# Free words between four SBUF buffers of a decoder trunk kernel: which matmul operands lie at which distance

## The chip, the cores and the metric

The kernel runs on one core of one Trainium2 chip. The metric is the device time of one execution in microseconds, taken from repeated runs of the same program; the profile is of one further execution. TensorE (PE in the profile) multiplies: one operand, 128 x 128 at most, is held in the array after a weight load (PEld), the other, up to 512 columns, is moved through it. VectorE (DVE) and ScalarE (ACT) work element by element, GpSimd (POOL) does a little of the same, and SyncE (SP) issues the transfers. SBUF is the on-chip memory with 128 partitions; addresses below are bytes within a partition, the same in all of them.

## What is computed

Two layers on 256 tokens of width 2048. Each has a token mixer (a state-space mixer in layer 0, a causal convolution in layer 1) and a SwiGLU network of inner width 5632. The dense parts are

```python
vg = y @ w_glu                                   # 2048 -> 2 x 2048, layer 0
ab = u @ w_pw1                                   # 2048 -> 2 x 2048, layer 1
return jax.nn.silu(v) @ w_pw2                    # 2048 -> 2048,     layer 1

def swiglu_ffn(u, w_gu, w_down):                 # both layers
    gu = u @ w_gu                                # 2048 -> 2 x 5632
    g, v = jnp.split(gu, 2, axis=-1)
    return (jax.nn.silu(g) * v) @ w_down         # 5632 -> 2048
```

with a layer norm and a modulation by a projection of the conditioning vector (`ada_w`) between them. All data are float32.

## The kernel before

**Products in parts.** Each dense product is made of three products in a rounded 32-bit matmul format: an operand x is split into a high part (x rounded to that format) and a low part (x minus the high part), and hi x hi, hi x lo and lo x hi are added in PSUM. So every weight and every activation lies in SBUF twice. `Unit` (L822) loads 512 rows by 512 columns of weights into a `raw` buffer, ScalarE writes the high part to `whi` (L830) and VectorE the low part to `wlo` (L831). Both tiles are 4 x 512 words and have two buffers each in one pool, `w` (L1392).

**The activations.** `h` (L1265) holds the 2048 input channels of a product, high and low, as 16 chunks x 2 x 256 words; it is written once for each mixer or network and read by all its panels. `f` is the tile `f2` of `ffn` (L1220), 24 chunks x 2 x 256 words, in the pools `f0` (L1531) and `f1` (L1682); it holds the inner values of the network for the down projection, and under the name `raw` (`entry_raw`, L1501) the inputs of the first panel after a norm.

**Which operand is held.** `gemm` (L838) walks over the units of four 128-row chunks. In the wide form (L886) a 128-token piece of h or f is held and a 512-column row of `whi` or `wlo` is moved; a unit has 16 matmuls on `whi`, with the high and the low part of the activations, and 8 on `wlo`, with the high part. In the last panel of each product the form is narrow (L890): 128 columns of `whi` or `wlo` are held and 256 tokens of h or f are moved. The first panel after a norm (`Entry.panel`, L992) has matmuls of the narrow kind with 258 columns (L1007), from rows of 258 words. Transposes (L902) bring the results of wide matmuls back to channels by tokens.

**What sets the order.** Weights come on SyncE's queue, one unit ahead and more; `Later` and `AdaQueue` put the modulation's products on VectorE (L699) at a fixed rate beside the units. Nothing of this order depends on addresses.

**Where the buffers lie.** Pools are stacked: each begins where the pool opened before it ends. Reading the addresses from the program that is built from the kernel before:

| tile | first byte | modulo 512 |
|---|---|---|
| h | 38272 | 384 |
| whi, two buffers of 8192 | 113344 | 192 |
| wlo, two buffers of 8192 | 129728 | 192 |
| pool s (statistics, gates, temporaries) | 146112 | 192 |
| f | 177088 | 448 |

A chunk's piece in h or f has 512 bytes, a row of `whi` or `wlo` 2048, a held piece of weights 512. So for wide and narrow matmuls the distance from the held to the moving operand, modulo 512, depends on the four first bytes alone. Moving minus held is 320 (wide, h), 256 (wide, f), 192 (narrow, h) and 256 (narrow, f).

Of the kernel before, what the change touches and what calls it, by code (L numbers as in the profile page):

```python
# [11 lines left out]
F32 = mybir.dt.float32  # L12
F32R = mybir.dt.float32r
# [6 lines left out]
P = 128  # L20
# [485 lines left out]
def kernel(  # L506
# [69 lines left out]
    def load_unit(src, k0, kn, segs, eng=nc.sync):  # L576

        r = raws[0].tile([P, 4, 512], F32, tag="raw", name="raw")
        if kn > 4:
            r = r.rearrange("p a b -> p (a b)").rearrange("p (k n) -> p k n", k=kn)  # L580
        raws.append(raws.pop(0))
        at = 0
        for c0, n in segs:
            eng.dma_start(r[:, :kn, at:at + n], src[k0 * P:(k0 + kn) * P, c0:c0 + n].rearrange("(k p) n -> p k n", p=P))
            at += n
        return r

    class Later:


        def __init__(self):
            self.now, self.todo = 0, []
# [17 lines left out]
    def queue_behind(instructions):  # L610

        st = ExitStack()
        for i in instructions:
            st.enter_context(tc.issue_after(i.ins))
        return st
# [206 lines left out]
    class Unit:  # L822


        def __init__(self, wp, wsrc, k0, kn, segs, behind=()):
            r = load_unit(wsrc, k0, kn, segs)
            self.hi = wp.tile([P, 4, 512], F32R, tag="whi", name="whi")
            self.lo = wp.tile([P, 4, 512], F32R, tag="wlo", name="wlo")
            with queue_behind([*behind, *held_back]):
                m1 = nc.scalar.copy(out=self.hi[:, :kn], in_=r[:, :kn])  # L830
                m2 = nc.vector.tensor_tensor(out=self.lo[:, :kn], in0=r[:, :kn], in1=self.hi[:, :kn].bitcast(F32), op=SUB)  # L831
            self.marks = [m1, m2]
            nonlocal newest
            newest = self
# [480 lines left out]
    w = s5.work  # L1315
# [70 lines left out]
    raws[:] = [rawp] * 4 + [more.enter_context(tc.tile_pool(name="raw5", bufs=2))] * 2  # L1386
    mctx = ExitStack()

    def start_dense():
        nonlocal const2, wp  # L1390
        const2 = ctx.enter_context(tc.tile_pool(name="const2", bufs=1, reuse_waits="tile"))
        wp = mctx.enter_context(tc.tile_pool(name="w", bufs=2, reuse_waits="tile"))  # L1392
        ready.append(Unit(wp, s5_w_glu[0], 0, 4, [(0, 256), (D, 256)]))

    const2 = wp = ln_col = wtap = fold32 = row_of = None
# [14 lines left out]
    with tc.manual_schedule(engines={mybir.EngineType.PE}):  # L1410
# [9 lines left out]
        for ct in range(NCH - 1):  # L1420
            now, y = coming, None
            if (ct + 1) % 4 == 1 and ct < 12:
                load_x(ct // 4 + 1)
            s5.weights_in(ct + 1)
            n = plan[ct + 1]
            ada_units(n > 0)
            with queue_behind([] if ct else [s5.made]):
                tabs[ct + 1] = s5.tables(ct + 1, [last])
            if held:
                y = s5.read_out(*held)  # L1430
            u, uh, last = inputs(ct + 1)
            ada_units(n > 1)
            coming = ct + 1, u, s5.drive(ct + 1, uh)
            if not ct:
                s5.weights_out(0, d_col[:, 0:1], last)
            s5.weights_out(ct + 1, d_col[:, ct + 1:ct + 2], last)
            ada_units(n - 2)
            if ct == NCH - 2:
                raws[:] = [rawp]
                more.close()  # L1440
                s5.keep_ctx.close()
                start_dense()
            scan(ct, now, y)
            if ct % 4 == 3 and ct < 11:
                extra = quarter_steps(ct // 4 + 2)
            with queue_behind([s5.last]):
                next(extra, None)
# [61 lines left out]
    with mctx:  # L1509
        sp = mctx.enter_context(tc.tile_pool(name="s", bufs=1, reuse_waits="tile"))  # L1510
        sp_ada = mctx.enter_context(tc.tile_pool(name="ada", bufs=1, reuse_waits="tile"))
        stats = Stats("ln00", sp)

        def enter(name, stats, i, k, raw, pairs):
# [197 lines left out]
```

## Time and profile before

| | us |
|---|---|
| median of three runs | 2320.72 |
| lowest and highest of them | 2317.39, 2323.02 |
| profiled execution, whole | 2323.75 |
| profiled execution, span from first to last instruction | 2322.0 |
| TensorE busy in the span | 2249.4 |
| VectorE busy | 1633.0 |
| ScalarE busy | 1011.1 |

TensorE's granted clock was 0.992 of full speed on the mean, and 1.00 in all stages from about 450 us on but the convolution. DMA moved 251 GB/s on the mean. A row of a group of instructions reads: line, engine, operation, output and inputs by the program's names, shapes, count, busy time, mean ns of one, idle time before them and what ended it. Matmuls are pipelined, and a duration holds the depth of the pipeline: a wide matmul lasts some 390 ns though the next one starts some 230 ns after it. The step between two is read from their starts.

### The profile page before, as it was taken

To read this page: it belongs to the slowest core of one execution; us is meant where nothing else is said; L and a number is where in the kernel's file an instruction comes from. 1 tells how busy PE (TensorE), PEld (TensorE's weight loads), DVE (VectorE), ACT (ScalarE), POOL (GpSimd) and SP (SyncE) were. 2 spreads that over 40 slices of the span, in tenths; PEclk is the share of its full clock that TensorE was granted. 3 is DMA by queue.
4 is the path that set the end of the run, shared out by engine and by line. 5 is a ranking of instruction groups with operands and counts; after the bars stand their busy time and mean duration, and the time that the engine had idled before them with its cause. 6 is when DMAs were issued, how large, how long until landed. Compare 5 with 4: busy or idle time off the path is not lost.

```text
span 2322.0 us, 33968 instructions
## 1 busy us (share of the span) xinstructions
PE 2249.4 (97%) x13905; PEld 1811.9 (78%) x13905; DVE 1633.0 (70%) x1778; ACT 1011.1 (44%) x1242; POOL 186.6 (8%) x283
## 2 busy tenths in 40 slices
PE   6888999999999999999999998999999999999998
PEld 4545778988888888888897676798888888888888
DVE  8899878887777777777885565788754544555564
ACT  4666335554333334344453322556434333334343
POOL 5662000000000000000011111400000000000000
PEclk9999999999999999999999999999999999999999
DMA  9889799589888898988757886766865556555542
GB/s 334 289 301 302 268 320 337 168 304 323 294 321 294 314 318 294 324 293 318 274 164 222 265 241 193 276 223 206 275 218 187 193 182 197 184 182 189 191 164 91
DMA packets 382307, 582.35 MB, mean 251 GB/s; under 512 B 13604, under 2 KB 279124, under 8 KB 367684
## 3 DMA queue, kind: packets, MB, share of 16 engines
q1 hardware_dynamic: 381718, 579.73, 73.8%
q8 instruction: 109, 1.79, 0.3%
q0 software_dynamic: 192, 0.37, 0.1%
q14 instruction: 48, 0.39, 0.0%
q10 hardware_dynamic: 240, 0.08, 0.0%
HBM read 575.97 MB, written 4.15 MB: 250 GB/s over the span
## 4 chain that ended last, share of the span: by engine, by line
PE 82%; DVE 8%; DMA 4%; ACT 3%; issue 1%; POOL 1%; SPq 0%; DVEq 0%; ACTq 0%; POOLq 0%
PE acc L886 67%; PE acc L890 5%; PE conv L1608 2%; DVE wlo L831 2%; PE acc L1007 2%; PE turned L902 2%; DMA raw<-in_cv_w_pw_dram 1%; DMA raw<-in_s_w_glu_dram 1%; ACT whi L830 1%; DVE pin L462 1%; PE y L499 1%; PE ada L628 1%; DMA raw<-in_ada_w_dram 1%; DVE adaacc L699 1%; DVE x L450 0%
## 5 line engine op out<-in xcount | busy, mean ns | idle before, releaser
L831 DVE TENSOR_TENSOR wlo<-raw,whi 128x2048 fp32r<-128x2048 f32 x344 | 795.6, 2313 | 491.0 <-ACT whi L830 490.6
L830 ACT CAST whi<-raw 128x2048 fp32r<-128x2048 f32 x344 | 655.0, 1904 | 805.0 <-PE acc L886 579.1
L886 PE MATMUL acc<-whi,h 128*128 128x512 f32 x3648 | 895.0, 395 | 10.8 <-ACT whi L830 10.5
L886 PEld LDWEIGHTS acc<-whi,h 128*128 128x128 f32 x3648 | 679.4, 188 | 169.7 <-ACT whi L830 16.4
L886 PE MATMUL acc<-wlo,h 128*128 128x512 f32 x1824 | 466.1, 392 | 2.8 <-DVE wlo L831 2.8
L886 PEld LDWEIGHTS acc<-wlo,h 128*128 128x128 f32 x1824 | 341.6, 188 | 81.3 <-DVE wlo L831 6.7
L886 PE MATMUL acc<-whi,f 128*128 128x512 f32 x1248 | 300.5, 391 | 0.0
L699 DVE SCALAR_TENSOR_TENSOR adaacc<-rawa,c_act,adaacc 128x2048 f32<-128x2048 f32 (+1 forms) x135 | 284.5, 2108 | 0.4
L886 PEld LDWEIGHTS acc<-whi,f 128*128 128x128 f32 x1248 | 233.0, 188 | 48.9 <-ACT whi L830 0.8
L886 PE MATMUL acc<-wlo,f 128*128 128x512 f32 x624 | 156.4, 389 | 0.0
L886 PEld LDWEIGHTS acc<-wlo,f 128*128 128x128 f32 x624 | 117.1, 188 | 24.3
L1581 POOL TENSOR_TENSOR lw<-fold,wtap 128x1024 f32<-128x1024 f32 x16 | 33.7, 2110 | 1146.4 <-PE acc L890 926.4
L628 PE MATMUL ada<-raw,c_rep 128*32 128x512 f32 (+1 forms) x576 | 72.5, 600 | 5.7 <-DMA raw<-in_ada_w_dram 3.2
L1240 ACT ACTIVATE fsg<-acc 128x256 f32<-128x256 f32 x84 | 31.7, 380 | 100.0 <-PE acc L886 100.0
L890 PEld LDWEIGHTS acc<-h,whi 128*128 128x128 f32 x512 | 62.1, 190 | 8.1 <-DVE h L1637 2.6
L890 PE MATMUL acc<-h,whi 128*128 128x256 f32 x512 | 65.7, 283 | 2.6 <-DVE h L1637 1.7
L1184 POOL CAST lnmh<-lno 128x2 fp32r<-128x2 f32 x1 | 0.2, 183 | 829.3 <-DVE lno L66 829.3
L1608 PE MATMUL conv<-vs,lw 128*32 128x256 f32 x1024 | 59.8, 380 | 0.0
L1608 PEld LDWEIGHTS conv<-vs,lw 128*32 128x32 f32 x1024 | 36.7, 110 | 20.9 <-issue 3.0
L1241 DVE TENSOR_TENSOR fsg<-acc,fsg 128x256 f32<-128x256 f32 x84 | 35.1, 420 | 19.9 <-ACT fsg L1240 19.8
L462 DVE TENSOR_TENSOR_SCAN pin<-rho,pin 128x256 f32<-128x256 f32 x64 | 44.3, 692 | 1.5
L1617 DVE SCALAR_TENSOR_TENSOR V<-conv,vec,shift 128x256 f32<-128x256 f32 x14 | 9.7, 693 | 48.8 <-PE conv L1608 48.8
(331 smaller groups left out, 1829.8 us busy)
## 6 DMA issues: line engine op xcount, KB each, us to landing
raw<-in_ffn_w_gu_dram SPq DMA_DIRECT2D x352, 512.0 KB, 4.5
rawa<-in_ada_w_dram SPq DMA_DIRECT2D x128, 1024.0 KB, 5.9
raw<-in_ffn_w_down_dram SPq DMA_DIRECT2D x88, 1024.0 KB, 5.1
raw<-in_ada_w_dram SPq DMA_DIRECT2D x64, 1024.0 KB, 7.8
raw<-in_s_w_glu_dram SPq DMA_DIRECT2D x64, 512.0 KB, 6.0
raw<-in_cv_w_pw_dram SPq DMA_DIRECT2D x64, 512.0 KB, 6.3
raw<-in_cv_w_pw_dram SPq DMA_DIRECT2D x16, 1024.0 KB, 5.6
vs<-scr SPq DMA_DIRECT2D x28, 284.0 KB, 7.4
```

The lines of the kernel that those rows point to most:

```text
L462: v.tensor_tensor_scan(out=z, data0=rh[:, a].rearrange("p r h c -> p (r h c)"), data1=z, initial=0.0, op0=MUL, op1=ADD)
L628: nc.tensor.matmul(acc[32 * (k % 4):32 * (k % 4) + 32, :], c_rep[:, kk, :], r[:, k, :], start=kk < 4, stop=kk >= NCH - 4)
L699: nc.vector.scalar_tensor_tensor(out=acc, in0=r[:, i], scalar=c_act[:, kk:kk + 1], in1=acc, op0=MUL, op1=ADD)
L830: m1 = nc.scalar.copy(out=self.hi[:, :kn], in_=r[:, :kn])
L831: m2 = nc.vector.tensor_tensor(out=self.lo[:, :kn], in0=r[:, :kn], in1=self.hi[:, :kn].bitcast(F32), op=SUB)
L886: nc.tensor.matmul(acc[bank].rearrange("p a b -> p (a b)"), x[:, bank * HALF:(bank + 1) * HALF], wt[:, k], start=first, stop=end)
L890: nc.tensor.matmul(acc[bank][:, i], wt[:, k, m * P:(m + 1) * P], x, start=first and i == 0, stop=end and i == 1)
L902: nc.tensor.transpose(b[:, o:o + HALF], u[t][:, c0 + k * P:c0 + (k + 1) * P], ident)
L1007: nc.tensor.matmul(acc[m][:, 0:EW], wt[:, k, m * P:(m + 1) * P], xx[:, 4 * u + k], start=u == 0 and n == 0, stop=u == 3 and n == len(order ...
L1241: nc.vector.tensor_tensor(out=t[:, i], in0=gv[:, 0], in1=t[:, i], op=MUL)
L1581: nc.gpsimd.tensor_tensor(out=lw, in0=fold32.unsqueeze(1).unsqueeze(1).broadcast_to([P, 4, CONV_G, 32]), in1=bc(wtap[:, :, 4 * ch:4 * ch + ...
L1608: nc.tensor.matmul(acc[32 * q:32 * q + 32, :], lw[:, q, g, :], vs[:, q, 4 * g:4 * g + SEQ], start=g == 0, stop=g == CONV_G - 1)
```

## The change

Three tiles that nobody writes or reads are put between pools: 48 words (192 bytes) before the pool of `whi`, 16 words (64 bytes) between `whi` and `wlo`, which get a pool each, and 16 words between the pool `ada` and the pools of f. Everything else in the kernel is as before.

```diff
         def __init__(self, wp, wsrc, k0, kn, segs, behind=()):
             r = load_unit(wsrc, k0, kn, segs)
-            self.hi = wp.tile([P, 4, 512], F32R, tag="whi", name="whi")
-            self.lo = wp.tile([P, 4, 512], F32R, tag="wlo", name="wlo")
+            self.hi = wp[0].tile([P, 4, 512], F32R, tag="whi", name="whi")
+            self.lo = wp[1].tile([P, 4, 512], F32R, tag="wlo", name="wlo")
...
+    def gap(c, n):
+
+        gaps.append(f"gap{len(gaps)}")
+        c.enter_context(tc.tile_pool(name=gaps[-1], bufs=1)).tile([P, n], F32, name=gaps[-1])
+
+    gaps = []
+
     def start_dense():
         nonlocal const2, wp
         const2 = ctx.enter_context(tc.tile_pool(name="const2", bufs=1, reuse_waits="tile"))
-        wp = mctx.enter_context(tc.tile_pool(name="w", bufs=2, reuse_waits="tile"))
+        gap(ctx, 48)
+        wp = [mctx.enter_context(tc.tile_pool(name="whi", bufs=2, reuse_waits="tile"))]
+        gap(mctx, 16)
+        wp.append(mctx.enter_context(tc.tile_pool(name="wlo", bufs=2, reuse_waits="tile")))
         ready.append(Unit(wp, s5_w_glu[0], 0, 4, [(0, 256), (D, 256)]))
...
         sp = mctx.enter_context(tc.tile_pool(name="s", bufs=1, reuse_waits="tile"))
         sp_ada = mctx.enter_context(tc.tile_pool(name="ada", bufs=1, reuse_waits="tile"))
+        gap(mctx, 16)
         stats = Stats("ln00", sp)
```

By the sizes of the free tiles, whi then begins at 113536, wlo at 129984, the pool s at 146368 and f at 177408; h stays at 38272.

## The prediction

> **What bounds the kernel now.** I read the page first: busy shares, then the chain of work that ended last; then the groups of instructions by shape, for the matmuls; then the timeline of TensorE, for the step from one matmul's start to the next; last the busy time by stage.
>
> ```profile
> span 2322.0 us, 33968 instructions
> ...
> PE 2249.4 (97%) x13905; PEld 1811.9 (78%) x13905; DVE 1633.0 (70%) x1778; ACT 1011.1 (44%) x1242; POOL 186.6 (8%) x283
> ...
> PE 82%; DVE 8%; DMA 4%; ACT 3%; issue 1%; POOL 1%; SPq 0%; DVEq 0%; ACTq 0%; POOLq 0%
> PE acc L886 67%; PE acc L890 5%; PE conv L1608 2%; DVE wlo L831 2%; PE acc L1007 2%; PE turned L902 2%; DMA raw<-in_cv_w_pw_dram 1%; DMA raw<-in_s_w_glu_dram 1%; ACT whi L830 1%; DVE pin L462 1%; PE y L499 1%; PE ada L628 1%; DMA raw<-in_ada_w_dram 1%; DVE adaacc L699 1%; DVE x L450 0%
> ```
>
> TensorE is busy for 97% of the span and holds 82% of the chain, and 67% of the chain is one line, L886: the wide matmuls, whose held operand is a 128-column piece of h or f and whose moving operand is a 512-column row of whi or wlo. So what counts is the step between two of them. The groups by shape (line, engine, operation, tiles, form, count, then busy time and mean ns of one) give the counts:
>
> ```profile
> L886 PE MATMUL acc<-whi,h 128*128 128x512 f32 x3648 | 895.0, 395 | 10.8 <-ACT whi L830 10.5
> L886 PE MATMUL acc<-wlo,h 128*128 128x512 f32 x1824 | 466.1, 392 | 2.8 <-DVE wlo L831 2.8
> L886 PE MATMUL acc<-whi,f 128*128 128x512 f32 x1248 | 300.5, 391 | 0.0
> L886 PE MATMUL acc<-wlo,f 128*128 128x512 f32 x624 | 156.4, 389 | 0.0
> L890 PE MATMUL acc<-h,whi 128*128 128x256 f32 x512 | 65.7, 283 | 2.6 <-DVE h L1637 1.7 <-ACT whi L830 0.7
> ...
> L890 PE MATMUL acc<-f,whi 128*128 128x256 f32 x320 | 40.7, 284 | 0.0
> L890 PE MATMUL acc<-h,wlo 128*128 128x256 f32 x256 | 33.6, 281 | 4.6 <-DVE wlo L831 4.6
> L1007 PE MATMUL acc<-raw,whi 128*128 128x258 f32 x256 | 33.3, 284 | 0.0
> ...
> L890 PE MATMUL acc<-f,wlo 128*128 128x256 f32 x160 | 21.2, 283 | 0.0
> ```
>
> Wide: 3648 + 1824 = 5472 on h and 1248 + 624 = 1872 on f. Narrow (L890, weights held, activations moving): 768 on h, 480 on f. One matmul's duration holds a pipeline's depth, so the step is read from starts. TensorE's timeline in the down projection (f held), start, us and count of each merged row:
>
> ```profile
> 708.06 1.98 PE L886 MATMUL acc<-wlo,f 128*128 128x512 f32 x8
> 709.87 3.79 PE L886 MATMUL acc<-whi,f 128*128 128x512 f32 x16
> 713.50 1.98 PE L886 MATMUL acc<-wlo,f 128*128 128x512 f32 x8
> 715.31 3.79 PE L886 MATMUL acc<-whi,f 128*128 128x512 f32 x16
> 718.94 1.98 PE L886 MATMUL acc<-wlo,f 128*128 128x512 f32 x8
> 720.75 1.98 PE L886 MATMUL acc<-whi,f 128*128 128x512 f32 x8
> ```
>
> From 708.06 to 720.75 are 56 matmuls in 12.69 us, a step of 226.6 ns. The same in the up projection (h held):
>
> ```profile
> 907.52 1.99 PE L886 MATMUL acc<-wlo,h 128*128 128x512 f32 x8
> 909.35 3.83 PE L886 MATMUL acc<-whi,h 128*128 128x512 f32 x16
> 913.01 1.99 PE L886 MATMUL acc<-wlo,h 128*128 128x512 f32 x8
> 914.84 1.99 PE L886 MATMUL acc<-whi,h 128*128 128x512 f32 x8
> 916.67 1.08 PE L886 MATMUL acc<-wlo,h 128*128 128x512 f32 x4
> 917.59 1.99 PE L886 MATMUL acc<-whi,h 128*128 128x512 f32 x8
> 919.42 1.08 PE L886 MATMUL acc<-wlo,h 128*128 128x512 f32 x4
> 920.34 3.83 PE L886 MATMUL acc<-whi,h 128*128 128x512 f32 x16
> 924.00 1.30 PE L886 MATMUL acc<-wlo,h 128*128 128x512 f32 x5
> ```
>
> From 907.52 to 924.00 are 72 matmuls in 16.48 us: 228.9 ns. Same shape, same clock, nobody waits, and 2.3 ns more. What differs is where the held operand lies. From the program's own allocation, bytes modulo 512: h 384, whi and wlo 192, f 448. So moving minus held is 320 for h and 256 for f, in every wide matmul, since all other offsets are multiples of 512. Narrow matmuls tell the same, with h moving (distance 192; the first two rows) and f moving (256):
>
> ```profile
> 1382.82 3.57 PE L890 MATMUL acc<-h,whi 128*128 128x256 f32 x30
> 1386.22 1.98 PE L890 MATMUL acc<-h,wlo 128*128 128x256 f32 x16
> ```
>
> ```profile
> 2280.76 2.80 PE L890 MATMUL acc<-f,whi 128*128 128x256 f32 x22
> 2283.40 2.08 PE L890 MATMUL acc<-f,wlo 128*128 128x256 f32 x16
> ```
>
> 3.40 us for 30 is 113.3 ns; 2.64 us for 22 is 120.0 ns. And 113.3 for 256 columns is half of 226.6 for 512: the two good cases agree on 0.443 ns a column. I take that for the floor of this data path; h in the wide form lies 2.3 ns above it, f in the narrow form 6.7.
>
> **The change, part by part.** No instruction, DMA, queue or order is added, removed or moved; there is no new wait. The three free tiles have 48, 16 and 16 words; nobody writes or reads them. whi moves by 192 bytes, wlo by 256, the f pool by 320; h stays. New residues: h 384, whi 384, wlo 448, f 256. Moving minus held becomes, in the wide form, whi on h 0, wlo on h 64, whi on f 128, wlo on f 192; in the narrow form h against whi 0, h against wlo 448, f against whi 384, f against wlo 320. Not one of the four wide distances occurs in the wide form of the trace of before, so their cost is unknown and is bounded from both sides.
>
> Better side: every wide matmul at the floor. On h 5472 x (228.9 - 226.6) = 12.6 us; f is there already, 0. Narrow f, 480 x 6.7 = 3.2 us; narrow h is at the floor in the row shown. Together 15.8 us. The panels (L1007) move 258 columns with rows of 258 words, so their distances wander through the residues before and after; I put 0.
>
> Worse side: the one step seen between a good and a bad distance is 120.0 - 113.3 = 6.7 ns per matmul. If all wide ones pay it, they come at 226.6 + 6.7 = 233.3: h 5472 x 4.4 = 24.1 us, f 1872 x 6.7 = 12.5 us, 36.6 us in all. By pair that is 16.1 (whi on h), 8.0 (wlo on h), 8.4 (whi on f), 4.2 (wlo on f).
>
> I take the floor for the wide pairs on h, because of the two wide distances seen one is at it and the other only 2.3 ns off, and because 128 columns are loaded there while 512 stream, against 256 in the narrow form: the wide one has more room. For f I take no change, for narrow ones none. How much of 12.6 us reaches the end is read by stage (window, its length, busy us and count of PE, PEld, DVE, ACT, POOL, granted clock, DMA share):
>
> ```profile
> 230.00:390.00 160.00, 155.48 (x733) 121.47 (x731) 135.39 (x118) 56.93 (x49) 3.03 (x2) 0.99 0.89 308
> ...
> 690.00:835.00 145.00, 145.00 (x664) 119.35 (x663) 105.19 (x66) 53.79 (x34) 0.00 (x0) 1.00 0.87 312
> 835.00:1060.00 225.00, 225.00 (x1013) 182.85 (x1013) 169.47 (x125) 87.70 (x72) 0.00 (x0) 1.00 0.87 306
> ```
>
> From 690 on TensorE has no hole, so a shorter step is a shorter span; DMA at 0.87 has 13% spare against 1% that a faster step asks. In the first dense stage it waits 4.5 us in 160, so about a tenth of the wide work sits where the gain may turn into a wait. 12.6 less some 1.5 is 11 us.
>
> One more part: DVE and ScalarE read and write the moved tiles. Residues of raw (384) and whi come to coincide in the subtraction on L831.
>
> ```profile
> L831 DVE TENSOR_TENSOR wlo<-raw,whi 128x2048 fp32r<-128x2048 f32 x344 | 795.6, 2313 | 491.0 <-ACT whi L830 490.6
> L699 DVE SCALAR_TENSOR_TENSOR adaacc<-rawa,c_act,adaacc 128x2048 f32<-128x2048 f32 x105 | 246.1, 2344 | 0.0
> ```
>
> L699 reads as many elements from two SBUF tiles at another distance (64 against 192) and takes 31 ns more: at most 344 x 31 = 10.7 us either way on an engine that idles 30% of the span, hidden behind the matmuls wherever PE has no hole. If that cover were gone, as in the first dense stage, a tenth of it, 1 us, would show. I put 0.
>
> **Sum.** The profiled execution took 2323.75 us (span 2322.0, 1.75 around it), 3.0 above the median of 2320.72. Less 11 gives 2312.8 for that execution and 2309.7 beside the median: 2310.
>
> **Rivals.** (1) *Distance is no cause.* The 2.3 ns could come from something else that h and f do not share, or the pairs may win and lose about the same: then 2321, between 2316 and 2326. The Trainium skill, "TensorE: Matmul & The Clock Gate", section "Step-by-step: what each phase is for", says that loading the next weights does not steal read bandwidth from the running matmul; "SBUF — State Buffer", section "Who interferes with whom", that PE waits on nobody. By those the layout is worth 0 us and the time stays 2321. Against it stand 120.0 and 113.3 ns for one instruction form, both with no wait; for it, that no run here moved one tile alone. That the free tiles are laid out otherwise than named falls here too.
>
> (2) *A collision on every wide matmul: slower.* The mechanism: while a row of the weights streams, the next piece of h or f is read; where both meet in the same part of the 512 bytes the stream stops for 6.7 ns, as in the narrow f rows. It decides pair by pair. whi on h alone costs 16 us (2337), both f pairs alone 12.5 (2333), all four 36.6 (2357). Speaking for it: f now sits at the floor and can only lose, and hi and lo, now at one distance, get two, so that at 16 and 8 matmuls the pattern has to settle anew. Against: 2.3 ns is the worst wide case seen. It becomes a loss once whi on h is off the floor by more than it is now.
>
> (3) *The floor is lower still.* Then both wide pairs gain. No row shows a 512-column step under 226.6, and half of it in another form agrees, so I price it by that agreement's error only: each ns under the floor is worth 7344 x 0.001 = 7.3 us, 2302 with the gain on h. The skill's "Back-to-back issue gap" on the same TensorE page gives N / 2.4 + 2.5 ns, 215.8 for 512 columns; by it an estimate would be 7344 x 10.8 = 79 us more, and no run here shows it.
>
> **Chances.** Forecast, wide on h at or near the floor (2303 to 2315): 0.42. Rival 1: 0.25. Rival 2: 0.25, most of it under 2340. Rival 3: 0.08. The range 2300 to 2340 holds the forecast, rival 1 and the cheaper half of rival 2, some 0.8. A measurement of this kernel tells 0.2%, about 4.6 us, from no change: faster 0.50 (forecast and rival 3), same 0.25, slower 0.25.
>
> **What would show it.** In the timeline of after, 24 wide matmuls from whi to the next whi take 5.44 us at the floor, 5.49 as now, 5.60 with a collision each, to be read for h and f apart; 30 narrow ones take 3.40 or 3.60. Mean durations of the four L886 groups move with it, by the same nanoseconds. Counts, DMA sizes and waits must be the same. The prediction is wrong if the step on h stays at 228.9, if the step on f rises, or if the gain on TensorE reappears as idle time before L886.

## The result and the profile after

The changed kernel takes 2335.70 us (median of 4 runs, 2332.44 to 2338.44); the kernel before, beside it, 2320.21 (4 runs, 2317.39 to 2323.02). The ratio is 1.0066, with a 95% interval of 1.0048 to 1.0084: **slower by 15.5 us**, 0.7%. The time lies in the range given; the forecast direction was wrong. The profiled execution of after took 2332.44 us, 3.3 under its median, where that of before, with 2323.75, lay 3.5 above this one (3.0 above the median of three that it was first set beside); so the two spans, 2322.0 and 2330.7, differ by only 8.7.

The page of after, the same lines as of before:

```profile
span 2330.7 us, 33968 instructions
...
PE 2263.3 (97%) x13905; PEld 1813.4 (78%) x13905; DVE 1634.5 (70%) x1778; ACT 1012.8 (43%) x1242; POOL 186.2 (8%) x283
...
PE 83%; DVE 9%; ACT 2%; DMA 2%; issue 2%; POOL 1%; SPq 0%; DVEq 0%; ACTq 0%; POOLq 0%
PE acc L886 67%; PE acc L890 5%; PE conv L1619 3%; DVE wlo L831 2%; PE acc L1007 2%; PE turned L902 2%; DVE pin L462 1%; ACT whi L830 1%; DVE adaacc L699 1%; PE y L499 1%; DMA raw<-in_s_w_glu_dram 1%; DMA raw<-in_cv_w_pw_dram 1%; PE ada L628 1%; DMA raw<-in_ada_w_dram 1%; DVE x L450 0%
```

Every count is the one of before, and the bound is the same. TensorE is busy 13.9 us longer (2263.3 - 2249.4) and idle 5.2 us less (67.4 against 72.6). That before idles more goes with the one execution of it that was profiled: a kernel with the same distances, shifted by 512 bytes (below), has 66.9 us of it in a span of 2316.7, and against that trace after is busy 13.5 us longer and idle 0.5 us longer.

```profile
PE 2249.8 (97%) x13905; PEld 1811.0 (78%) x13905; DVE 1632.6 (70%) x1778; ACT 1010.4 (44%) x1242; POOL 186.0 (8%) x283
```

So no wait has taken the place of another: the matmuls themselves come more slowly. The groups of TensorE by shape (line, engine, operation, tiles, form, count, then busy us and mean ns of one, then idle time and its releasers) show which:

```profile
L886 PE MATMUL acc<-whi,h 128*128 128x512 f32 x3648 | 890.3, 393 | 8.0 <-ACT whi L830 7.7
L886 PE MATMUL acc<-wlo,h 128*128 128x512 f32 x1824 | 471.1, 395 | 2.9 <-DVE wlo L831 2.9
L886 PE MATMUL acc<-whi,f 128*128 128x512 f32 x1248 | 306.6, 396 | 0.0
L886 PE MATMUL acc<-wlo,f 128*128 128x512 f32 x624 | 160.1, 394 | 0.0
...
L890 PE MATMUL acc<-h,whi 128*128 128x256 f32 x512 | 68.0, 288 | 2.0 <-DVE h L1648 1.0 <-ACT whi L830 0.9
...
L890 PE MATMUL acc<-f,whi 128*128 128x256 f32 x320 | 40.3, 283 | 0.0
...
L890 PE MATMUL acc<-h,wlo 128*128 128x256 f32 x256 | 34.1, 284 | 4.3 <-DVE wlo L831 4.3
...
L890 PE MATMUL acc<-f,wlo 128*128 128x256 f32 x160 | 20.8, 280 | 0.0
```

Beside before's rows, whi on h went from 395 to 393 ns, wlo on h from 392 to 395, whi on f from 391 to 396, wlo on f from 389 to 394, narrow h against whi from 283 to 288 and against wlo from 281 to 284. One wide pair gained and three lost; of the narrow pairs those with h lost, and those with f gained a little (284 to 283 and 283 to 280). The timeline of TensorE (start us, length us, then the group and its count) gives the steps. In the down projection, f held:

```profile
709.29 2.03 PE L886 MATMUL acc<-wlo,f 128*128 128x512 f32 x8
711.16 3.88 PE L886 MATMUL acc<-whi,f 128*128 128x512 f32 x16
714.87 2.03 PE L886 MATMUL acc<-wlo,f 128*128 128x512 f32 x8
```

From 709.29 to 714.87 are 24 matmuls in 5.58 us, 232.5 ns each where they were 226.6. In the up projection, h held:

```profile
907.92 3.80 PE L886 MATMUL acc<-whi,h 128*128 128x512 f32 x16
911.56 2.01 PE L886 MATMUL acc<-wlo,h 128*128 128x512 f32 x8
913.41 1.99 PE L886 MATMUL acc<-whi,h 128*128 128x512 f32 x8
915.23 1.10 PE L886 MATMUL acc<-wlo,h 128*128 128x512 f32 x4
916.17 2.00 PE L886 MATMUL acc<-whi,h 128*128 128x512 f32 x8
918.01 1.10 PE L886 MATMUL acc<-wlo,h 128*128 128x512 f32 x4
918.94 3.81 PE L886 MATMUL acc<-whi,h 128*128 128x512 f32 x16
```

The first 16 on whi take 3.64 us, 227.5 ns each, nearly the floor. The next 8 on wlo take 1.85 us, 231.3 ns, above the 228.9 of before; the two runs of 4 take 0.94 and 0.93, about 234. So the cost is highest in the first matmuls after a change from whi to wlo, and where the runs are short these are all there are.

A mean step for each pair, for all of the trace, can be worked out from the starts of successive matmuls. A wide matmul's step runs to the start of the next wide one, whichever pair that belongs to; a narrow one's runs from the start of the narrow one before it. Steps of 260 ns and more are left out, so that waits and other work between them stay out. For the narrow form this limit is wide, and some waits stay in. The whole account of the change is this:

| pair | count | distance before, after | step before, ns | step after, ns | count x difference, us |
|---|---|---|---|---|---|
| wide, whi on h | 3648 | 320, 0 | 229.27 | 228.54 | -2.7 |
| wide, wlo on h | 1824 | 320, 64 | 228.90 | 231.83 | +5.3 |
| wide, whi on f | 1248 | 256, 128 | 227.20 | 232.21 | +6.3 |
| wide, wlo on f | 624 | 256, 192 | 226.68 | 232.85 | +3.9 |
| narrow, h against whi | 512 | 192, 0 | 119.31 | 124.51 | +2.7 |
| narrow, h against wlo | 256 | 192, 448 | 118.99 | 119.82 | +0.2 |
| narrow, f against whi | 320 | 256, 384 | 120.94 | 119.75 | -0.4 |
| narrow, f against wlo | 160 | 256, 320 | 120.00 | 117.91 | -0.3 |

The sum is +15.0 us, against 15.5 measured. With steps under 160 ns alone narrow h against whi goes from 115.9 to 119.8, worth 2.0 us and not 2.7; the kernel shifted by 512 bytes has 114.5 there, at the distance of before. So the narrow rows of the table are known to a microsecond or so, the wide ones better: between before and the shifted kernel their steps agree within 0.1 ns.

### The profile page after: what moved, and what is told of

The parts are those of the page before. It is cut to its first block, busy times and chain, and to the rows that moved or that the text cites. A ratio compares the mean times of both kernels' runs of the same rounds, so it can differ in the third digit from the quotient of the medians.

```text
span 2330.7 us, 33968 instructions
## 1 busy us (share of the span) xinstructions
PE 2263.3 (97%) x13905; PEld 1813.4 (78%) x13905; DVE 1634.5 (70%) x1778; ACT 1012.8 (43%) x1242; POOL 186.2 (8%) x283
## 4 chain that ended last, share of the span: by engine, by line
PE 83%; DVE 9%; ACT 2%; DMA 2%; issue 2%; POOL 1%; SPq 0%; DVEq 0%; ACTq 0%; POOLq 0%
PE acc L886 67%; PE acc L890 5%; PE conv L1619 3%; DVE wlo L831 2%; PE acc L1007 2%; PE turned L902 2%; DVE pin L462 1%; ACT whi L830 1%; DVE adaacc L699 1%; PE y L499 1%; DMA raw<-in_s_w_glu_dram 1%; DMA raw<-in_cv_w_pw_dram 1%; PE ada L628 1%; DMA raw<-in_ada_w_dram 1%; DVE x L450 0%
## 5 line engine op out<-in xcount | busy, mean ns | idle before, releaser
L831 DVE TENSOR_TENSOR wlo<-raw,whi 128x2048 fp32r<-128x2048 f32 x344 | 795.6, 2313 | 495.1 <-ACT whi L830 492.9
L886 PE MATMUL acc<-wlo,h 128*128 128x512 f32 x1824 | 471.1, 395 | 2.9 <-DVE wlo L831 2.9
L886 PE MATMUL acc<-whi,f 128*128 128x512 f32 x1248 | 306.6, 396 | 0.0
L886 PEld LDWEIGHTS acc<-whi,f 128*128 128x128 f32 x1248 | 233.7, 188 | 54.6 <-ACT whi L830 0.8
```

Of the source, the lines that this page charges most:

```text
L886: nc.tensor.matmul(acc[bank].rearrange("p a b -> p (a b)"), x[:, bank * HALF:(bank + 1) * HALF], wt[:, k], start=first, stop=end)
```

## The experiments

Three theories stood to be told apart. First, that the step depends on the **distance** from held to moving operand, pair by pair, with some period. Second, that it depends on something else that the free words move with them: the absolute place, or the pools being separate. Third, that two distances in alternation cost something **as such**, whatever they are. (A fourth stood in the expectations of the first runs, that any shift of the weights against h costs; the first run below, which is faster, ends it.) In all kernels the weights have a pool each and `gap` is as in the change; only the numbers of free words differ (ahead of whi, between whi and wlo, ahead of f), but for the last one. The short diffs are against the changed kernel. Steps in the tables are worked out as above.

**Only the first gap.** h and f keep one distance each: 0 for h, 256 for f.

```diff
         gap(ctx, 48)
...
-        gap(mctx, 16)
         wp.append(mctx.enter_context(tc.tile_pool(name="wlo", bufs=2, reuse_waits="tile")))
...
-        gap(mctx, 16)
         stats = Stats("ln00", sp)
```

> Only the 48 words before whi are left of the change. Residues: h 384, whi and wlo 384, f 128; moving minus held in the wide form 0 on h, 256 on f. Theory A (the residue of moving minus held modulo 512 sets the step; 0 and 256 settle at 226.7 ns in the traces of after and before): every wide matmul at 226.7 ns, so 5472 x (228.9 - 226.7) = 12 us below the kernel before, less up to 3 us because narrow matmuls on h go from 113 to 118 ns to some 120; about 2310. Theory B (the loss comes from giving whi and wlo two distances, whatever they are): as the kernel before, 2320. Theory C (any shift of the weights against h costs): slower than before, up to 2335.

Measured: 2312.37 us against 2318.78, ratio 0.9979 (0.9970 to 0.9989): this part alone is 6.4 us **faster**. Its timeline with h held:

```profile
908.07 1.98 PE L886 MATMUL acc<-whi,h 128*128 128x512 f32 x8
909.89 1.07 PE L886 MATMUL acc<-wlo,h 128*128 128x512 f32 x4
910.79 1.98 PE L886 MATMUL acc<-whi,h 128*128 128x512 f32 x8
912.61 1.07 PE L886 MATMUL acc<-wlo,h 128*128 128x512 f32 x4
913.51 3.79 PE L886 MATMUL acc<-whi,h 128*128 128x512 f32 x16
```

24 matmuls from 908.07 to 913.51 take 5.44 us, 226.7 ns: distance 0 is at the floor, and without a second distance the runs of 4 are at it too. The wide pairs on h gain 3648 x 1.75 + 1824 x 2.01 = 10.1 us by their mean steps (227.52 and 226.89), and narrow h gives back 512 x 5.2 + 256 x 3.7 = 3.6 (3.0 by the steps under 160 ns).

**Only the last gap.** f moves by 64 bytes, h and the weights lie as before; f's distance becomes 192, h's stays 320.

```diff
-        gap(ctx, 48)
...
-        gap(mctx, 16)
         wp.append(mctx.enter_context(tc.tile_pool(name="wlo", bufs=2, reuse_waits="tile")))
...
         gap(mctx, 16)
         stats = Stats("ln00", sp)
```

> Only the 16 words before the pools of f are left of the change. Residues: h 384, whi and wlo 192, f 0; moving minus held 320 on h as before, 192 on f for whi and wlo alike. Theory A: wide matmuls on h stay at 228.9 ns, those on f go from 226.7 to the 233.3 ns that wlo shows on f in the trace of after: 1872 x 6.6 = 12.4 us slower, narrow ones on f between 113 and 120 ns instead of 120, up to 3 us back; 2330 to 2333. Theory B (two distances for whi and wlo cost): no change, 2320. Theory C (only the weights against h matter): no change.

Measured: 2330.89 against 2318.78, 1.0054 (1.0042 to 1.0066), 12.1 us slower. Its timeline with f held:

```profile
706.51 3.89 PE L886 MATMUL acc<-whi,f 128*128 128x512 f32 x16
710.25 2.03 PE L886 MATMUL acc<-wlo,f 128*128 128x512 f32 x8
712.12 3.89 PE L886 MATMUL acc<-whi,f 128*128 128x512 f32 x16
```

24 matmuls in 5.61 us, 233.8 ns by these rounded starts; the mean over the trace is 233.3 on both whi and wlo. The steps on h stay at 229.3 and 228.9. By the steps, f costs 1248 x 6.12 + 624 x 6.63 = 11.8 us. Of the operands of the wide matmuls only f was moved here, which is the held one (the pool of the convolution, opened behind the same gap, moved with it); the matmuls that hold f slowed, and no others of the wide ones.

**All by 512 bytes** (`gap(ctx, 128)`, no other gap): the distances of before, at other places and in separate pools.

```diff
-        gap(ctx, 48)
+        gap(ctx, 128)
...
-        gap(mctx, 16)
...
-        gap(mctx, 16)
```

> One gap of 128 words (512 bytes) before whi and none else: all addresses of weights, pool s and f move, every distance modulo 512 is that of the kernel before. Theory A: each wide step as before, 228.9 on h and 226.7 on f, time 2320 within 5 us. If the period were 1024 or more, or if absolute addresses counted, steps on h and on f against the weights could change (f moves along with the weights, h does not): then the step on h leaves 228.9 and that on f stays.

Measured: 2318.51 against 2318.78, 1.0004 (0.9995 to 1.0014); wide steps 229.27, 228.86, 227.18 and 226.71, those of before. Separate pools and a free tile cost nothing by themselves.

**Distance 256 for both** (`gap(ctx, 112)`, no other gap): h and f both at 256, which before had for f alone.

```diff
-        gap(ctx, 48)
+        gap(ctx, 112)
...
-        gap(mctx, 16)
...
-        gap(mctx, 16)
```

> One gap of 112 words before whi. Residues: h 384, whi and wlo 128, f 384; moving minus held 256 in all wide pairs and in all narrow pairs. Theory A: all wide matmuls at 226.7 ns (12 us less than before), all narrow ones at 120.0 ns (768 on h from 113 to 118 up to 120, 3 us more): about 2311. Theory B: as before, 2320. Theory C: slower than before.

Measured: 2312.63 against 2318.78, 0.9977 (0.9968 to 0.9985). Steps on h 227.57 and 226.87, on f 227.07 and 226.66. For the wide form 256 is as good as 0 was, and h at f's distance has f's step.

**Only the middle gap** (`gap(mctx, 16)` between whi and wlo alone): whi on h 320, wlo on h 384, whi on f 192, wlo on f 256.

```diff
-        gap(ctx, 48)
...
         gap(mctx, 16)
         wp.append(mctx.enter_context(tc.tile_pool(name="wlo", bufs=2, reuse_waits="tile")))
...
-        gap(mctx, 16)
         stats = Stats("ln00", sp)
```

> Only the 16 words between whi and wlo are left of the change. Residues: h 384, whi 192, wlo 256, f 0; wide distances 320 (whi on h), 384 (wlo on h), 192 (whi on f), 256 (wlo on f). Theory A (each pair has its own step, set by its own distance): whi on f 233.3 ns, wlo on f close to 226.7 after three or four settling steps at each switch, whi on h near 229, wlo on h unknown; on f alone 1248 x 6.6 = 8 us slower, total 2326 to 2336. Rival B (it is the difference between whi and wlo as such that costs, whichever distances they have): both f pairs lose about alike, some 5 ns each, as in the trace of after.

Measured: 2331.02 against 2319.65, 1.0053 (1.0036 to 1.0070), 11.4 us slower. Steps 229.76, 232.01, 233.28 and 229.54. wlo on f keeps its distance of 256 and still comes 2.9 ns later than in before: what it pays for is the change from whi at 192.

```profile
708.58 2.00 PE L886 MATMUL acc<-wlo,f 128*128 128x512 f32 x8
710.41 3.89 PE L886 MATMUL acc<-whi,f 128*128 128x512 f32 x16
```

Here 8 on wlo take 1.83 us, 228.8 ns, where 8 took 1.81 in before. The sum of the steps gives +16.7 us here, more than was measured, and just outside the interval; more on that below.

**More distances, without alternation.** Three kernels give h and f one distance each, most of them new. The diff is the first one's, h 64 and f 128; h 384 with f 448 has 16 words ahead of whi and 80 ahead of f, h 32 with f 288 has 56 and 120.

```diff
-        gap(ctx, 48)
+        gap(ctx, 64)
...
-        gap(mctx, 16)
         wp.append(mctx.enter_context(tc.tile_pool(name="wlo", bufs=2, reuse_waits="tile")))
...
-        gap(mctx, 16)
+        gap(mctx, 32)
```

> Gaps of 64 words before whi and 32 before f; whi and wlo alike. Wide distance 64 on h, 128 on f. Theory A with period 512: no forecast for 64 alone; 128 near the 232 ns that whi on f has in the trace of after. Theory A with period 256 (0 and 256 gave the same 226.7): 64 behaves as 320, steady 228.9 ns. Against it stand the 231.8 ns of wlo on h at 64 in the trace of after, which settling at each switch could explain. Time: period 256, on h nothing and on f 1872 x 5 = 9 us slower, 2328; else up to 2342.

> Gaps of 16 words before whi and 80 before f; whi and wlo alike. Wide distance 384 on h, 448 on f. Period 256: 384 as 128, some 232 ns, and 448 as 192, 233.3 ns: 5472 x 3 + 1872 x 6.6 = 29 us slower, 2348. Period 512: steps that no run has shown so far.

> Gaps of 56 words before whi and 120 before f; whi and wlo alike. Wide distance 32 on h, 288 on f; in the narrow form 480 and 224. It asks whether steps are set in units finer than 64 bytes. Period 256: 32 and 288 give one and the same step. If the unit is 64 bytes, 32 behaves as 0 or as 64, 226.7 or about 229 ns. If finer, a third value; a step below 226.6 would show that this is no floor.

Measured: h 64 and f 128 take 2330.32 against 2319.65, 1.0038 (1.0019 to 1.0057); h 384 and f 448 take 2345.67, 1.0112 (1.0091 to 1.0132); h 32 and f 288 take 2351.50, 1.0135 (1.0118 to 1.0151), the slowest of all. The timeline of the first, with h held at 64:

```profile
914.37 1.99 PE L886 MATMUL acc<-wlo,h 128*128 128x512 f32 x8
916.20 1.99 PE L886 MATMUL acc<-whi,h 128*128 128x512 f32 x8
```

8 on wlo take 1.83 us, 228.8 ns: the distance of wlo on h in the changed kernel, without the alternation. There the mean was 231.8, here it is 228.9, so 3 ns of it is the change from one distance to the other. With h at 384:

```profile
911.60 3.88 PE L886 MATMUL acc<-whi,h 128*128 128x512 f32 x16
915.32 2.03 PE L886 MATMUL acc<-wlo,h 128*128 128x512 f32 x8
917.18 2.02 PE L886 MATMUL acc<-whi,h 128*128 128x512 f32 x8
```

24 in 5.58 us, 232.5 ns; f at 128, in the kernel before this one, has 232.6. With h at 32:

```profile
918.91 3.89 PE L886 MATMUL acc<-whi,h 128*128 128x512 f32 x16
922.65 2.03 PE L886 MATMUL acc<-wlo,h 128*128 128x512 f32 x8
924.51 2.03 PE L886 MATMUL acc<-whi,h 128*128 128x512 f32 x8
```

24 in 5.60 us, 233.3 ns. 32 bytes off the best distance is as bad as 192.

**Two distances, both good** (48 and 64 words, none ahead of f): whi at 0 and wlo at 256, on h and on f.

```diff
         gap(ctx, 48)
...
-        gap(mctx, 16)
+        gap(mctx, 64)
         wp.append(mctx.enter_context(tc.tile_pool(name="wlo", bufs=2, reuse_waits="tile")))
...
-        gap(mctx, 16)
         stats = Stats("ln00", sp)
```

> Gaps of 48 words before whi and 64 words (256 bytes) between whi and wlo, none before f. Wide distances: whi on h 0, wlo on h 256, whi on f 0, wlo on f 256; so whi and wlo have two distances as in the change, but both of the kind that settles at 226.7 ns. Theory A with period 256 (runs so far: 0 and 256 alike, 64 and 320, 128 and 384, 192 and 448, 32 and 288): no settling at the switches, every wide matmul at 226.7, narrow ones at 120; 2312 to 2314, as with the first gap only. Rival B (two distances as such cost): steps of 231 to 233 ns for some of the four pairs as in the trace of after, and 2325 or more.

Measured: 2312.20 against 2319.36, 0.9966 (0.9953 to 0.9979). Steps 227.55, 226.85, 227.12, 226.71, those of the kernel with one distance. Its timeline:

```profile
909.87 1.98 PE L886 MATMUL acc<-whi,h 128*128 128x512 f32 x8
911.68 1.07 PE L886 MATMUL acc<-wlo,h 128*128 128x512 f32 x4
912.59 1.98 PE L886 MATMUL acc<-whi,h 128*128 128x512 f32 x8
914.40 1.07 PE L886 MATMUL acc<-wlo,h 128*128 128x512 f32 x4
915.30 3.79 PE L886 MATMUL acc<-whi,h 128*128 128x512 f32 x16
```

24 in 5.43 us, with four changes from one distance to the other. Alternation as such costs nothing. Where a cost showed, the two distances have steps 2 ns or more apart: 0 with 64 on h in after (1.0 ns on whi, 3.0 on wlo), 192 with 256 on f in the middle gap alone (2.9 ns on wlo); 320 with 384 on h there puts 0.5 ns on whi and takes 0.5 off wlo. Where both are slow and less than 1 ns apart, 128 with 192 on f in after, there was none: 232.21 and 232.85, against 232.6 and 233.3 by themselves.

**The narrow form too.** Wide pairs at 0 or 256, and narrow panels' whi written 16 words further into its tile, so that a narrow pair with whi lies at 192 or 448 (the longer tile puts the two buffers 256 bytes apart, modulo 512).

```diff
-        def __init__(self, wp, wsrc, k0, kn, segs, behind=()):
+        def __init__(self, wp, wsrc, k0, kn, segs, behind=(), at=0):
...
-            self.hi = wp[0].tile([P, 4, 512], F32R, tag="whi", name="whi")
+            self.hi = wp[0].tile([P, 2112], F32R, tag="whi", name="whi")[:, at:at + 2048].rearrange("p (k n) -> p k n", n=512)
...
-                w = Unit(wp, wsrc, k0 + u0, kn, segs, feed.marks if feed and u == 1 else ())
+                w = Unit(wp, wsrc, k0 + u0, kn, segs, feed.marks if feed and u == 1 else (), 0 if wide else 16)
...
-        gap(mctx, 16)
         wp.append(mctx.enter_context(tc.tile_pool(name="wlo", bufs=2, reuse_waits="tile")))
...
-        gap(mctx, 16)
         stats = Stats("ln00", sp)
```

> A version meant to beat both kernels: the gap of 48 words before whi alone, and in the panels of the narrow form the high part of the weights is written 16 words further on in its tile (which gets 64 words more), so that the narrow distance from held whi is 448 on h and 192 on f instead of 0 and 256, while all wide distances stay at 0 or 256. Theory A: wide at 226.7 ns, narrow on whi from 120 to between 113 and 118 ns, some 800 x 3.5 = 3 us less than with the first gap only: about 2309. Rival (narrow steps do not follow the distance but what ran before them): 2312, narrow steps at 120.

Measured: 2308.61 against 2319.36, 0.9953 (0.9939 to 0.9967), 10.8 us faster than before and **the fastest of all**. Its interval overlaps that of the kernel just above it on the same chip, so the last 3.6 us between these two are not shown by the times; the steps show some 2 of them. Narrow h in the kernel with the first gap alone, at distance 0:

```profile
1372.81 4.00 PE L890 MATMUL acc<-h,whi 128*128 128x256 f32 x32
1376.64 2.08 PE L890 MATMUL acc<-h,wlo 128*128 128x256 f32 x16
```

and here:

```profile
1371.99 3.93 PE L890 MATMUL acc<-h,whi 128*128 128x256 f32 x32
1375.76 2.08 PE L890 MATMUL acc<-h,wlo 128*128 128x256 f32 x16
```

3.83 us for 32 is 119.7 ns, 3.77 is 117.8. Over the trace narrow h against whi falls from a mean of 124.5 to 119.1, narrow f against whi from 120.9 to 118.4. By the steps under 160 ns, which leave waits out, it is 119.8 to 116.8 and 119.8 to 117.4: 512 x 3.0 + 320 x 2.4 = 2.3 us.

Put together, for the wide form and without alternation:

| distance, bytes modulo 512 | step, ns | seen in |
|---|---|---|
| 0 and 256 | 226.7 | before (f), first gap alone, 256 for both, two good distances |
| 64 and 320 | 228.9 | before (h), h 64 |
| 128 and 384 | 232.5 | f 128, h 384 |
| 192 and 448 | 233.3 | last gap alone, f 448 |
| 32 and 288 | 233.3 | h 32, f 288 |

The figures are those of wlo and of both pairs on f. whi on h has 0.4 to 0.9 ns more in the first two lines (227.5 at 0 and 256, 229.3 at 64 and 320). Distances 256 bytes apart agree in each line, h and f agree at one distance, and so do different absolute places (f at 192 and 448 begins at residue 0 and 320, h at 64 and 320 has whi at residue 448 and 192). So the first theory holds for the wide form, with a period of **256 bytes**; the second and third fall.

Where the steps say more than the time: h 384 with f 448 sums to 31.7 us by its steps, 26.0 were measured (21 to 31 by the interval); h 32 with f 288 to 35.8, 31.9 were measured (27 to 35); the middle gap alone to 16.7 against 11.4. In after, the sum and the time agree. That the rest is hidden in the stages where TensorE has holes is not shown: against the kernel shifted by 512 bytes TensorE's busy time rises by 29.5, 30.9 and 12.9 us in these three, each inside the interval of the time, and its idle time (64.3, 72.6 and 66.7 us) lies near the 66.9 and 72.6 of the two traces with before's distances. So the sums of steps say some microseconds too much, and why stays open.

## Why the prediction was wrong, step by step

**The bound: right.** TensorE set the time in all twelve kernels, and the readings of 226.6, 228.9 and 120.0 ns in before's timeline were ones of distance. The 113.3 was not of distance alone: the same pair, narrow h against whi at 192, has another steady pace in the same trace.

```profile
408.23 3.93 PE L890 MATMUL acc<-h,whi 128*128 128x256 f32 x32
```

The next row begins at 412.00; 3.77 us for 32 is 117.8 ns. So the floor that the prediction took from two forms that agree rests, for the narrow one, on the better of two paces at one distance. Rival 1, that distance is no cause, falls with the last gap alone: one held tile moved by 64 bytes, and 1872 matmuls went from about 227 to 233.3 ns. The Trainium skill states that loading the next weights takes no read bandwidth from the running matmul ("TensorE: Matmul & The Clock Gate", section "Step-by-step: what each phase is for") and that PE waits on nobody ("SBUF — State Buffer", section "Who interferes with whom"). That a layout is worth nothing, as the prediction's rival drew from these, does not hold in this kernel: where the held operand lies changes the pace of the stream by up to 6.6 ns in 233.3. Whether it is the load that slows the stream is not shown, as the records show the pace alone.

**The step that failed** is the choice "I take the floor for the wide pairs on h, because of the two wide distances seen one is at it and the other only 2.3 ns off", with "For f I take no change, for narrow ones none" behind it, for which no reason is given. Two distances out of the possible ones, 226.6 and 228.9, were taken for the span of the wide form. They were its best and its second best; the others are at 232.5 and 233.3. The argument that the wide form has more room, since 128 columns are loaded while 512 stream, is wrong in size: a bad distance costs a wide matmul 6.6 ns, as much as the narrow form's 6.7. Of the forecast's 12.6 us on h, 0 on f and 0 on the narrow ones, the runs show:

- *whi on h: -8.4 forecast (two thirds of 12.6, by the counts), -2.7 measured.* Distance 0 is at the floor, as forecast (226.7 in the first gap alone), but in after its pace is broken by wlo at 64: the mean is 228.54, against 227.52 with the same distance and no alternation. That difference is 3.7 us.
- *wlo on h: -4.2 forecast, +5.3 measured.* 64 has the step of 320, 228.9, so nothing was to be gained; the alternation adds 3 ns, 5.4 us.
- *f: 0 forecast, +10.2 measured.* 128 and 192 are two of the bad distances.
- *narrow: 0 forecast, +2.2 measured.* Here the worst distance is the best of the wide form: 0 and 256 settle at 120.0. The 113.3 of one timeline row was taken for all of narrow h; before's mean is 119.3, so its cost to 0 is 5.2 ns by the table, and 3.8 by the steps under 160 ns, less than the 6.7 that the row suggested.

**Rival 2 was what happened**, in its terms and nearly in its price. It said that f "now sits at the floor and can only lose": its 12.5 us for both f pairs are 10.2 in after and 11.8 by the steps of the last gap alone. It said that "hi and lo, now at one distance, get two, so that at 16 and 8 matmuls the pattern has to settle anew": 9.1 us (3.7 and 5.4). It put 36.6 us on all four wide pairs in collision, and h 32 with f 288, where that is the case, lost 31.9. Its point of decision was wrong: it had whi on h turn the sign, and whi on h was the one pair that gained. And its picture, that a loss arises where load and stream "meet in the same part of the 512 bytes", is not borne out: equal places, distance 0, are the best of the wide form, and the period is 256. That 2335.70 lies inside the range of 2300 to 2340 is owed to the share that rival 2 had in it, and not to the mechanism that was forecast.

**Rival 3: not seen.** No mean step of a wide pair in any kernel is under 226.6 ns.

**VectorE and ScalarE: right at 0.** The row of after for the subtraction that was feared:

```profile
L831 DVE TENSOR_TENSOR wlo<-raw,whi 128x2048 fp32r<-128x2048 f32 x344 | 795.6, 2313 | 495.1 <-ACT whi L830 492.9 <-PE acc L886 2.0
```

2313 ns as before, to the digit, though the residues of raw and whi now coincide. The panels on L1007, put at 0, have 284 ns in both.

**How much reaches the end.** The windows of the dense stages (length, busy us and count of PE, PEld, DVE, ACT, POOL, granted clock, DMA share):

```profile
690.00:835.00 145.00, 145.00 (x650) 116.96 (x649) 103.18 (x63) 51.27 (x31) 0.00 (x0) 1.00 0.85 304
835.00:1060.00 225.00, 225.00 (x1010) 182.33 (x1009) 168.96 (x126) 88.53 (x73) 0.00 (x0) 1.00 0.87 304
```

TensorE has no hole there, as before, and the clock is the same; in the first window, f's, it does 650 matmuls where it did 664, 2.1% less work in the same time. That is the change, read without a single step. The prediction's "From 690 on TensorE has no hole" is too wide: in before it is busy 192.98 us of 1200 to 1400 and 67.70 of 1400 to 1480. Whether the forecast's discount of 1.5 us is right is not settled, as the idle time of two traces with the same distances differs by more (66.9 and 72.6).

Against what was to be seen: 24 wide matmuls take 5.44 us at distance 0, 5.49 in after on h and 5.58 on f, between the marks 5.44, 5.49 and 5.60 that were set. The prediction named both signs of its failure, a step on h that stays and a step on f that rises; both came.

## What to carry to other kernels

Where TensorE is the bound and held and moving operands both stream from SBUF, read the step from successive starts for each pair of tiles and compare like shapes: a few ns between them can be the tiles' distance, and one free tile is enough to test it. Try every distance that a pair can have before choosing one, as two that happen to occur say nothing of the rest, and keep all pairs that alternate at distances with the same step. Change one tile's place at a time: the first gap here was worth 6.4 us of gain, and came in one change with gaps that lost more than three times that.

## What the hardware showed that was not expected

- The step of a 512-column matmul in this kernel's 32-bit format, with a new 128-column held piece each time, depends on the distance of the two operands modulo 256 bytes, from 226.7 to 233.3 ns, 2.9%; 32 bytes are enough to go from the best to the worst that was seen.
- The 256-column form has it the other way round: distances 0 and 256 settle at 120.0 ns, the others seen are mostly a little lower (320 in after 117.9 on the mean). One distance can have more than one steady step: narrow h against whi at 192 has rows with 113.3 and rows with 117.8 ns. In before its median is 117, in the kernel shifted by 512 bytes, at the same distance, 114. So for this form the distance alone does not settle the step.
- The pace has a memory. After a change to a distance with another step it takes several matmuls to settle: whi on h in after, at a distance worth 226.7 ns, comes at up to 236 in the first five and only then at 227 (in runs of 16 the means by place are 230.2, 233.7, 229.8, 229.5, 228.5, then 226.9 and less). A steady pace can also be a cycle: the 228.9 of before is made of steps of about 230.2, 228.0 and 228.7 ns, over and over. Between two distances with the same step there is no such cost (5.43 us for 24).
- Left open: what inside the chip meets what, why wide and narrow differ, what chooses between the two paces of the narrow form, and the other distances (96, 160 and 224, and all that are no multiple of 32 bytes). None of these was tried.
